# Issuing the sums, high parts and activation parts of a wide step ahead of the low parts of the step before it, in a fused attention, recurrence and feed-forward block

## The chip, the cores and the metric

The kernel runs on one core of a Trainium2 chip. A core has five engines with an instruction queue each: TensorE multiplies matrices, VectorE and ScalarE work on elements, GpSimd has little to do here, and SyncE issues most transfers from the chip's memory. Each engine works through its queue in order; across engines, an instruction waits on semaphores. The metric is the time of one execution in microseconds of the device, as the median of several runs.

## The reference, cut to what matters

One decoder layer on 256 positions of width 2048, in 32-bit floats. A norm, one combined projection, a dilated window attention and a gated recurrence, two branch projections with gates, an output projection and a residual; then

```
a = rmsnorm(h, norm_ffn_pre)
gt, up = split(a @ w_ffn_gate_up, [5632])      # 2048 x 11264
ff = (silu(gt) * up) @ w_ffn_down              # 5632 x 2048
h = h + rmsnorm(ff, norm_ffn_post)
```

The change lies in the feed-forward part alone, the last 690 us of the execution.

## The kernel before, in words

**Split products.** Every 32-bit number x is written as hi + lo, two numbers in TensorE's own 32-bit format. ScalarE makes `hi` by a copy into that format, VectorE makes `lo` as x - hi, and a product takes three matmuls: hi by hi, hi by lo and lo by hi. So each weight that TensorE uses costs a copy on ScalarE and a subtraction on VectorE first, the latter waiting for the former.

**Narrow and wide steps.** All projections up to the first block of the feed-forward go in chunks of 128 x 1024 elements (`load`, `split`, `multiply`, lines 210 to 272; the copy is L242, the subtraction L243). From the second gate/up block on the work goes in wide steps of 128 x 2048: two row blocks of 128 times two column groups of 512. There are ten gate/up blocks of 8 wide steps (`GATE_UP`) and two down blocks of 22 (`DOWN`).

**Plain and by7 steps.** A plain wide step is 24 matmuls of 512 columns. A by7 step computes its 2 by 2 block product with seven products instead of eight (21 matmuls) and pays for that with sums: three VectorE instructions over the weight (L310, L316, L317, tile `sum`), the high part of these in two halves (L315, L318, tile `w`), and a second pair of high and low parts for the plain weight (`dh` L320, `dl` L322), beside the low part of the sums (`wl` L321). A plain step has one high part (`w` L305) and one low part (`wl` L306). Steps 2, 4 and 6 of a gate/up block are by7, steps 4, 7, ..., 19 of the first down block and 3, 6, ..., 18 of the second.

**Activations.** In gate/up all activation parts exist beforehand. In down, `prep_act` makes them step by step: a high part on ScalarE (L410) and a low part on VectorE (L411, tile `a`), and for a by7 step four sums on VectorE (L379 to L383, tile `s`), their high part on ScalarE (L384) and their low part on VectorE (L385, tile `so`).

**Between blocks.** When a block's last by7 step is multiplied, `gather` (L363) spreads the four extra products: a copy on ScalarE (L367) and four additions on VectorE (L368 to L371, tile `e`). When the block is done, `evac_ffn` adds the banks (L1151), applies the gate's function (L1154) and multiplies gate and up (L1157); after step 1 of the next block TensorE transposes the outcome (L1117 in `turn_act`) into the activations of down. A down block's `evac_down` adds (L1191), squares and applies the gain (L1200).

**Buffers.** `raw` (a weight as loaded) has three buffers, `w` (high parts) three, `wl` (low parts) three, `sum`, `dh` and `dl` one each. A buffer is written again when all users of the tile that it held before are done, whatever the order in which the instructions were written down: step n's high part waits on ScalarE for TensorE to finish step n-3, and the load of step n waits on SyncE for the last reader of `raw` of step n-3, which is `wl` (L306) in a plain step and `dl` (L322) in a by7 step.

**Order.** It is written out by hand. For each wide step i the loop issues: `split_wide(i + 2)`, which holds all the preparation of step i + 2; the load of step i + 5 (two transfers of 512 KB); the matmuls of step i; `gather`, the next piece of the evacuation, the transposes, where they fall on this step. At the end the last three steps are multiplied side by side, so that the two halves of the output can be finished one after the other.

Of the kernel before, what the change touches and what calls it, by code (L numbers as in the profile page):

```python
# [13 lines left out]
F32 = mybir.dt.float32  # L14
F32R = mybir.dt.float32r
I32 = mybir.dt.int32
AF = mybir.ActivationFunctionType
OP = mybir.AluOpType

P = 128  # L20
# [57 lines left out]
def tile_hybrid_block(ctx: ExitStack, tc: tile.TileContext, t, out):  # L78
    nc = tc.nc
# [12 lines left out]
    def nm(s):  # L92
        serial[0] += 1
        return f"{s}_{serial[0]}"

    def rslot(s):
        return rpool.tile([P, 1024], F32R, tag="r", bufs=16, name=nm(s))
# [10 lines left out]
    def p3(s, dtype, n, bufs, tag=None):  # L108
        return act_pool[0].tile([P, n], dtype, tag=tag or s, bufs=bufs, name=nm(s))
# [73 lines left out]
    blocks, chunks, pairs = [], [], []  # L183
    wides, steps = [], []
# [21 lines left out]
    def parts(j):  # L206

        return (slice(0, 512), slice(512, 1024)) if j == 0 else (slice(0, 1024),)
# [19 lines left out]
    def wslot():  # L228
        return stream.tile([P, 2048], F32R, tag="w", bufs=N_SPLIT, name=nm("w"))

    def split(j, only=None):
        if j >= len(chunks):
            split_wide(j - len(chunks))
            return
        raw = chunks[j][2]
        if chunks[j][3] is None:
            w = wslot()
            chunks[j][3:] = [w[:, :1024], w[:, 1024:]]
        wh, wl = chunks[j][3:]
        for n, k in enumerate(parts(j)):  # L240
            if only in (None, n):
                nc.scalar.activation(wh[:, k], raw[:, k], AF.Copy)  # L242
                nc.vector.tensor_sub(wl[:, k], raw[:, k], wh[:, k].bitcast(F32))  # L243
# [48 lines left out]
            )  # L292
        steps[n][2] = raw

    def split_wide(n):

        if n >= len(steps):
            return
        b, i, raw = steps[n][:3]
        m, by7 = b.order[i]  # L300
        if b.prep:
            b.prep(m, by7)
        hi, lo = wslot(), p3("wl", F32R, 2048, 3)
        if not by7:
            nc.scalar.activation(hi, raw, AF.Copy)  # L305
            nc.vector.tensor_sub(lo, raw, hi.bitcast(F32))  # L306
            steps[n][3] = hi, lo
            return
        s, d = p3("sum", F32, 2048, 1), raw[:, 512:]
        nc.vector.tensor_sub(  # L310
            s[:, :1024].rearrange("p (a c) -> p a c", a=2),
            raw[:, 512:1536].rearrange("p (a c) -> p a c", a=2),
            raw[:, None, :512].to_broadcast([P, 2, 512]),
        )
        nc.scalar.activation(hi[:, :1024], s[:, :1024], AF.Copy)  # L315
        nc.vector.tensor_add(s[:, 1024:1536], raw[:, 512:1024], s[:, 512:1024])  # L316
        nc.vector.tensor_sub(s[:, 1536:], raw[:, 1536:], s[:, 1024:1536])  # L317
        nc.scalar.activation(hi[:, 1024:], s[:, 1024:], AF.Copy)  # L318
        dhi, dlo = p3("dh", F32R, 1536, 1), p3("dl", F32R, 1536, 1)
        nc.scalar.activation(dhi, d, AF.Copy)  # L320
        nc.vector.tensor_sub(lo, s, hi.bitcast(F32))  # L321
        nc.vector.tensor_sub(dlo, d, dhi.bitcast(F32))  # L322
        steps[n][3] = hi, lo, dhi, dlo
# [50 lines left out]
    def seven_sums(f, dst):  # L374

        s = ptile("s").rearrange("p (n t) -> p n t", n=4)
        a11, a12, a21, a22 = f[:, 0, :P], f[:, 1, :P], f[:, 0, P:], f[:, 1, P:]
        for o, x, c, y in ((0, a21, -1.0, a22), (1, s[:, 0, :], -1.0, a11)):
            nc.vector.scalar_tensor_tensor(  # L379
                out=s[:, o, :], in0=x, scalar=c, in1=y, op0=OP.mult, op1=OP.subtract  # L380
            )
        nc.vector.tensor_sub(s[:, 2, :], a11, a21)
        nc.vector.tensor_sub(s[:, 3, :], a12, s[:, 1, :])  # L383
        nc.scalar.activation(dst[:, 0], s, AF.Copy)  # L384
        nc.vector.tensor_sub(dst[:, 1], s, dst[:, 0].bitcast(F32))  # L385

    def sums_of(dst):
        return lambda n: (dst[:, 0, n, :], dst[:, 1, n, :])


    class Split:
# [14 lines left out]

        def put(self, n, src):

            x = self.slots[n]
            nc.scalar.activation(x[:, :, 0, :], src, AF.Copy)  # L410
            nc.vector.tensor_sub(x[:, :, 1, :], src, x[:, :, 0, :].bitcast(F32))  # L411
            self.there.add(n)

# [158 lines left out]
    def start():  # L572
        keep_warm(WARM)
        ps = aux()
        nc.tensor.transpose(ps[:, :16], rowg[:16], ident[:16, :16])
        nc.vector.tensor_copy(colg[:, :16], ps[:, :16])
        high, low = transpose_in(xt, colg, xT, 0, True)
        for kk in range(2):
            high(kk)
            low(kk)  # L580
            split(0, kk)
        keep_warm(BRIDGE)
        transpose_in(xt, colg, xT, 1)
        lanes[0].append(opening())
# [579 lines left out]
    fss, fz, fpost, parts_of, a7 = [], {}, [], {}, {}  # L1164
# [8 lines left out]
                t["norm_ffn_post"][:, j * 1024 : (j + 1) * 1024].to_broadcast([P, 1024]),  # L1173
            )

    def prep_act(m, by7):
        f = act_t[m // 2][:, m % 2 * 2 : m % 2 * 2 + 2, :]
        x = parts_of[m] = Split("a", 2)
        x.put(0, f)
        if by7:  # L1180
            dst = rslot("so").rearrange("p (z n t) -> p z n t", z=2, n=4)
            seven_sums(f, dst)
            a7[m] = sums_of(dst)
# [95 lines left out]
    for half in range(2):  # L1279
# [3 lines left out]
        for g in range(3):  # L1283
            c = 1024 * g + 512 * half
# [22 lines left out]
    for j in range(2):  # L1307
        add_wide_block(t["w_ffn_down"][0], (1024 * j, 1024 * j + 512), DOWN[j], act,
                       lambda m: a7[m], evac_down, prep=prep_act,
                       pre=begin_down if j == 0 else None, turn=3 if j == 0 else None)  # L1310
# [5 lines left out]
    for j in range(1, 4):  # L1316
        load_x(j)
        load(2 * j)
        if j < 3:
            load(2 * j + 1)  # L1320
    start()
    split(1)
    for j in range(N_RAW + 1, N_RAW + AHEAD):
        load(j)
    for i in range(len(chunks)):
        b, c = chunks[i][:2]
        if c == 0 and b.pre:
            b.pre()
        split(i + AHEAD)
        load(i + AHEAD + N_RAW)  # L1330
        multiply(i)
        if b.post:
            b.post(c)
        advance(evacs)
        if turns and type(turns[0]) is not list:
            advance(turns)
        for lane in lanes:
            advance(lane)
        if c == b.steps - 1:
            evacs.append(b.evac(b.banks))  # L1340
# [3 lines left out]
    for i in range(len(steps)):  # L1344
        b, c = steps[i][:2]
        now[0] = b
        if c == 0 and b.pre:
            b.pre()
        split_wide(i + AHEAD)
        load_wide(2 * (i + AHEAD + N_RAW // 2))  # L1350
        if i >= len(steps) - 3:
            continue
        multiply_wide(i)
        if c == b.last7:
            gather(b)
        advance(evacs)
        if c == b.turn:
            flush(evacs)
            turn_act(turns.popleft())
        if c == len(b.order) - 1:  # L1360
            evacs.append(b.evac(b))
            advance(evacs)
# [63 lines left out]
```

## Time and profile before

| what | value |
|---|---|
| median of 3 runs | 1753.54 us (1752.17 to 1753.55) |
| the profiled execution, own time | 1753.68 us |
| its span, first to last instruction | 1751.9 us |
| TensorE busy | 1730.3 us, 99% |
| VectorE busy | 1265.1 us, 72% |
| ScalarE busy | 885.0 us, 51% |
| loaded from memory | 322.40 MB, 185 GB/s over the span |

In the profile's rows, PE is TensorE's matmuls, PEld its loads of weights, DVE is VectorE, ACT ScalarE, SP SyncE. A timeline row gives start and duration in microseconds, engine, line, operation, the tile written and the tiles read, the shape, how many instructions are merged, and, in brackets, how long the engine had been idle and what ended that. Instructions overlap a little at their ends, so the next one can start some 0.08 us before the duration is over. A row by stretches gives the stretch, its length, then busy time and instructions of PE, PEld, DVE, ACT and POOL, the granted TensorE clock, the busy share of the DMA engines and GB/s.

### The profile page before, as it was taken

Reading aid. Unit: us, or ns where it says so; the run is one execution under the profiler, and the core shown is the slowest. Engines: PE = TensorE matmul, PEld = TensorE weight load, DVE = VectorE, ACT = ScalarE, POOL = GpSimd, SP = SyncE. Lnnn points to the kernel's source line nnn. Section 1 sums busy time; section 2 is a strip of 40 time slices with the busy share of each in tenths; the row PEclk is TensorE's granted clock in tenths of the full one; section 3 lists DMA queues with packets and bytes.
Section 4 is the critical chain, followed back from the end, with each engine's and each line's share of the span. In section 5 each row is a group of like instructions: output and inputs, shape, how many; then the busy total and the mean of one; then the engine's idle time right before and its main releaser. Section 6 shows DMA issues by size and latency. Waiting matters only on the chain.

```text
span 1751.9 us, 21592 instructions
## 1 busy us (share of the span) xinstructions
PE 1730.3 (99%) x8424; PEld 1449.0 (83%) x8424; DVE 1265.1 (72%) x1372; ACT 885.0 (51%) x1050; POOL 74.1 (4%) x54
## 2 busy tenths in 40 slices
PE   9999999999999999999999999999999999999997
PEld 7888888888888888888888877888888888878775
DVE  5657657877546775544565577888888888888887
ACT  6545445344444444454444465555555555565563
POOL 0002404300000000000000000000000000000000
PEclk9999999999999999999999999999999999999999
DMA  7655444455455554455555745555555555656553
GB/s 265 204 191 193 144 162 151 145 165 182 159 169 169 189 188 161 159 175 193 194 183 189 268 157 203 194 192 193 204 206 204 201 194 192 223 181 218 183 183 117
DMA packets 201223, 325.92 MB, mean 186 GB/s; under 512 B 10096, under 2 KB 76832, under 8 KB 201120
## 3 DMA queue, kind: packets, MB, share of 16 engines
q1 hardware_dynamic: 198848, 319.41, 54.2%
q10 hardware_dynamic: 2272, 5.12, 0.8%
q8 instruction: 66, 1.08, 0.2%
q14 instruction: 37, 0.30, 0.1%
HBM read 322.40 MB, written 2.10 MB: 185 GB/s over the span
## 4 chain that ended last, share of the span: by engine, by line
PE 82%; DVE 12%; ACT 3%; issue 2%; DMA 1%; POOL 0%; SPq 0%; DVEq 0%; ACTq 0%
PE acc L115 65%; PE aux L115 16%; DVE wl L306 3%; DVE wl L321 1%; DVE dl L322 1%; DVE a L411 1%; DVE sum L310 1%; ACT w L318 1%; DVE w L243 1%; DVE sum L317 0%; DVE sum L316 0%; ACT w L242 0%; DVE w L667 0%; ACT so L384 0%; DVE s L379 0%
## 5 line engine op out<-in xcount | busy, mean ns | idle before, releaser
L243 DVE TENSOR_TENSOR w<-raw,w 128x1024 fp32r<-128x1024 f32 (+1 forms) x353 | 444.2, 1260 | 366.4 <-ACT w L242 364.3
L242 ACT ACTIVATE w<-raw 128x1024 fp32r<-128x1024 f32 (+1 forms) x353 | 373.0, 1057 | 483.1 <-PE acc L115 472.1
L115 PE MATMUL acc<-w,xT 128*128 128x512 f32 x1728 | 407.9, 394 | 0.0
L115 PEld LDWEIGHTS acc<-w,xT 128*128 128x128 f32 x1728 | 325.1, 190 | 65.7 <-DVE w L243 0.3
L115 PE MATMUL acc<-xT,w 128*128 128x512 f32 (+1 forms) x2048 | 365.5, 340 | 0.0
L115 PEld LDWEIGHTS acc<-xT,w 128*128 128x128 f32 x2048 | 314.8, 189 | 46.1
L306 DVE TENSOR_TENSOR wl<-raw,w 128x2048 fp32r<-128x2048 f32 x82 | 187.4, 2285 | 19.9 <-ACT w L305 19.9
L305 ACT ACTIVATE w<-raw 128x2048 fp32r<-128x2048 f32 x82 | 156.4, 1908 | 59.0 <-PE aux L115 27.0
L115 PE MATMUL acc<-w,hT 128*128 128x512 f32 x622 | 182.5, 392 | 1.5 <-DVE w L243 1.2
L115 PEld LDWEIGHTS acc<-w,hT 128*128 128x128 f32 x622 | 115.8, 188 | 27.0 <-DVE w L243 2.5
L115 PE MATMUL aux<-w,hT 128*128 128x512 f32 x430 | 135.6, 389 | 0.0
L321 DVE TENSOR_TENSOR wl<-sum,w 128x2048 fp32r<-128x2048 f32 x42 | 96.3, 2292 | 47.3 <-ACT w L318 47.3
L115 PEld LDWEIGHTS aux<-w,hT 128*128 128x128 f32 x430 | 80.7, 188 | 16.8
L315 ACT ACTIVATE w<-sum 128x1024 fp32r<-128x1024 f32 x42 | 44.6, 1063 | 96.3 <-DVE sum L310 92.0
L115 PE MATMUL acc<-w,yT 128*128 128x512 f32 x384 | 88.0, 390 | 0.2 <-DVE w L243 0.2
L115 PEld LDWEIGHTS acc<-w,yT 128*128 128x128 f32 x384 | 71.9, 188 | 15.4 <-DVE w L243 0.6
L115 PE MATMUL acc<-w,a 128*128 128x512 f32 x268 | 83.7, 389 | 0.0
L115 PE MATMUL aux<-w,a 128*128 128x512 f32 x268 | 83.7, 389 | 0.0
L115 PE MATMUL aux<-wl,hT 128*128 128x512 f32 x215 | 83.6, 389 | 0.0
L115 PE MATMUL acc<-wl,hT 128*128 128x512 f32 x215 | 83.6, 389 | 0.0
L322 DVE TENSOR_TENSOR dl<-raw,dh 128x1536 fp32r<-128x1536 f32 x42 | 73.5, 1751 | 0.0
L320 ACT ACTIVATE dh<-raw 128x1536 fp32r<-128x1536 f32 x42 | 61.9, 1473 | 0.0
(263 smaller groups left out, 2016.9 us busy)
## 6 DMA issues: line engine op xcount, KB each, us to landing
raw<-in_w_in SPq DMA_DIRECT2D x271, 512.0 KB, 4.5
raw<-in_w_ffn_gate_up SPq DMA_DIRECT2D x176, 512.0 KB, 4.4
raw<-in_w_ffn_down SPq DMA_DIRECT2D x88, 512.0 KB, 4.9
raw<-in_w_mix_out SPq DMA_DIRECT2D x32, 512.0 KB, 4.9
raw<-in_w_attn_branch SPq DMA_DIRECT2D x16, 512.0 KB, 4.6
raw<-in_w_hgrn_branch SPq DMA_DIRECT2D x16, 512.0 KB, 4.6
hx<-in_x ACTq DMA_DIRECT2D x4, 512.0 KB, 9.9
x<-in_x SPq DMA_DIRECT2D x3, 512.0 KB, 10.4
```

The lines of the kernel that those rows point to most:

```text
L115: nc.tensor.matmul(ps, lhsT, rhs, start=start, stop=stop, skip_group_check=True)
L242: nc.scalar.activation(wh[:, k], raw[:, k], AF.Copy)
L243: nc.vector.tensor_sub(wl[:, k], raw[:, k], wh[:, k].bitcast(F32))
L305: nc.scalar.activation(hi, raw, AF.Copy)
L306: nc.vector.tensor_sub(lo, raw, hi.bitcast(F32))
L310: nc.vector.tensor_sub(s[:, :1024].rearrange("p (a c) -> p a c", a=2), raw[:, 512:1536].rearrange("p (a c) -> p a c", a=2), raw[:, None, : ...
L315: nc.scalar.activation(hi[:, :1024], s[:, :1024], AF.Copy)
L318: nc.scalar.activation(hi[:, 1024:], s[:, 1024:], AF.Copy)
L320: nc.scalar.activation(dhi, d, AF.Copy)
L321: nc.vector.tensor_sub(lo, s, hi.bitcast(F32))
L322: nc.vector.tensor_sub(dlo, d, dhi.bitcast(F32))
L411: nc.vector.tensor_sub(x[:, :, 1, :], src, x[:, :, 0, :].bitcast(F32))
```

## The change

`split_wide(n)` is cut in two. The new `front(n)` makes the activation's high part, the sums and the high parts of a step, and then the rest of its activation parts. `split_wide(n)` now makes `dh` of step n, then calls `front(n + 1)`, and then makes the low parts of step n. So the sums, high parts and activation parts of step n + 1 stand in the queues of VectorE and ScalarE ahead of the low parts of step n, and `front(i + 3)` is issued in the turn of step i, before the matmuls of step i. All three sums now come ahead of both halves of the high part, and in a by7 step of down the activation's low part and its seven sums come behind the weight's sums. The very first `front` is issued ahead of the split of the last narrow chunk. No buffer is added, the loads and the matmuls keep their order, and no instruction is added or taken away.

```diff
     def split(j, only=None):
+        if j >= len(chunks) - 1 and only is None:
+            split_wide(j - len(chunks))
         if j >= len(chunks):
-            split_wide(j - len(chunks))
             return
...
-    def split_wide(n):
+    def front(n):
 
         if n >= len(steps):
             return
         b, i, raw = steps[n][:3]
         m, by7 = b.order[i]
         if b.prep:
-            b.prep(m, by7)
-        hi, lo = wslot(), p3("wl", F32R, 2048, 3)
+            b.prep(m)
+        hi = wslot()
         if not by7:
             nc.scalar.activation(hi, raw, AF.Copy)
+            steps[n][3] = raw, hi
+        else:
+            s, d = p3("sum", F32, 2048, 1), raw[:, 512:]
+            nc.vector.tensor_sub(
+                s[:, :1024].rearrange("p (a c) -> p a c", a=2),
+                raw[:, 512:1536].rearrange("p (a c) -> p a c", a=2),
+                raw[:, None, :512].to_broadcast([P, 2, 512]),
+            )
+            nc.vector.tensor_add(s[:, 1024:1536], raw[:, 512:1024], s[:, 512:1024])
+            nc.vector.tensor_sub(s[:, 1536:], raw[:, 1536:], s[:, 1024:1536])
+            nc.scalar.activation(hi[:, :1024], s[:, :1024], AF.Copy)
+            nc.scalar.activation(hi[:, 1024:], s[:, 1024:], AF.Copy)
+            steps[n][3] = s, hi, d
+        if b.prep:
+            b.prep(m, by7)
+
+    def split_wide(n):
+
+        by7 = 0 <= n < len(steps) and steps[n][0].order[steps[n][1]][1]
+        if by7:
+            dhi = p3("dh", F32R, 1536, 1)
+            nc.scalar.activation(dhi, steps[n][3][2], AF.Copy)
+        front(n + 1)
+        if n >= len(steps) or n < 0:
+            return
+        if not by7:
+            raw, hi = steps[n][3]
+            lo = p3("wl", F32R, 2048, 3)
             nc.vector.tensor_sub(lo, raw, hi.bitcast(F32))
             steps[n][3] = hi, lo
             return
...
+        s, hi, d = steps[n][3]
+        dlo, lo = p3("dl", F32R, 1536, 1), p3("wl", F32R, 2048, 3)
         nc.vector.tensor_sub(lo, s, hi.bitcast(F32))
         nc.vector.tensor_sub(dlo, d, dhi.bitcast(F32))
...
-    def prep_act(m, by7):
+    def prep_act(m, by7=None):
+
         f = act_t[m // 2][:, m % 2 * 2 : m % 2 * 2 + 2, :]
-        x = parts_of[m] = Split("a", 2)
-        x.put(0, f)
+        if by7 is None:
+            parts_of[m] = Split("a", 2)
+            parts_of[m].high(0, f)
+            return
+        parts_of[m].low(0, f)
         if by7:
```

`put` of `Split` is cut into `high` (the copy on ScalarE) and `low` (the subtraction on VectorE) for this, and calls both where it is used otherwise.

More of the change, by code (lines that the diff above doesn't have):

```diff
@@ L308, in split_wide @@
             return
[L309 to L320, printed above, removed]
+        s, hi, d = steps[n][3]
+        dlo, lo = p3("dl", F32R, 1536, 1), p3("wl", F32R, 2048, 3)
         nc.vector.tensor_sub(lo, s, hi.bitcast(F32))
@@ L407, in put, with high, low @@
         def put(self, n, src):
+            self.high(n, src)
+            self.low(n, src)
+        def high(self, n, src):
+            nc.scalar.activation(self.slots[n][:, :, 0, :], src, AF.Copy)
+        def low(self, n, src):
             x = self.slots[n]
-            nc.scalar.activation(x[:, :, 0, :], src, AF.Copy)
             nc.vector.tensor_sub(x[:, :, 1, :], src, x[:, :, 0, :].bitcast(F32))
```

## The prediction, as put on record before the run

> **What bounds the kernel now.** I read the page first, then busy time by stretches, the chain of waits, and last the timelines of single engines around the steps that the change moves.
>
> ```profile
> span 1751.9 us, 21592 instructions
> ...
> PE acc L115 65%; PE aux L115 16%; DVE wl L306 3%; DVE wl L321 1%; DVE dl L322 1%; DVE a L411 1%; DVE sum L310 1%; ACT w L318 1%; DVE w L243 1%; DVE sum L317 0%; DVE sum L316 0%; ACT w L242 0%; DVE w L667 0%; ACT so L384 0%; DVE s L379 0%
> ```
> The chain belongs to TensorE for 81%; the VectorE lines in it are those that the change moves. By stretches, gate/up (1066 to 1501 us) and down (from 1501) differ:
>
> ```profile
> 1400.00:1500.00 100.00, 100.00 (x451) 82.99 (x450) 87.40 (x71) 54.61 (x46) 0.00 (x0) 1.00 0.60 204
> 1500.00:1600.00 100.00, 98.70 (x435) 80.25 (x434) 86.31 (x95) 57.17 (x57) 0.00 (x0) 1.00 0.61 200
> ```
> In gate/up TensorE is full: nothing can be won there. In down it waits, at one place per three steps:
>
> ```profile
> 1556.53 0.50 PE L115 MATMUL aux<-dl,a 128*128 128x512 f32 x1 [0.28 <-DVE dl L322]
> 1572.74 0.50 PE L115 MATMUL aux<-dl,a 128*128 128x512 f32 x1 [0.27 <-DVE dl L322]
> 1654.66 0.50 PE L115 MATMUL acc<-dl,a 128*128 128x512 f32 x1 [1.61 <-DVE dl L322]
> ```
> Three down steps take 16.21 us. Their 24+24+21 matmuls need, by the next row (48 in 10.88 us, 0.2267 each; 5.44 for a plain step, 4.76 for a by7 step), 15.64. So 0.57 is lost per cycle; nine such cycles, 0.5 at the first by7 step (a row further down) and 1.9 at 1654.66 (each is the idle time in brackets and 0.3 for the slower first matmuls behind it) make **7.5 us**: the most that a faster supply could give.
>
> ```profile
> 1458.62 10.88 PE acc L115 x48
> ```
> What holds the supply is VectorE's own order:
>
> ```profile
> 1557.00 2.28 DVE L306 TENSOR_TENSOR wl<-raw,w 128x2048 fp32r<-128x2048 f32 x1
> 1559.20 0.68 DVE L411 TENSOR_TENSOR a<-act,a 128x512 fp32r<-128x512 f32 x1
> ...
> 1562.01 0.68 DVE L411 TENSOR_TENSOR a<-act,a 128x512 fp32r<-128x512 f32 x1
> 1562.61 0.28 DVE L379 SCALAR_TENSOR_TENSOR s<-act 128x128 f32<-128x128 f32 x1
> ...
> 1564.32 0.69 DVE L385 TENSOR_TENSOR so<-s,so 128x512 fp32r<-128x512 f32 x1 [0.70 <-ACT so L384]
> 1564.93 1.22 DVE L310 TENSOR_TENSOR sum<-raw 128x1024 f32<-128x1024 f32 x1
> ...
> 1566.90 0.69 DVE L317 TENSOR_TENSOR sum<-raw,sum 128x512 f32<-128x512 f32 x1
> 1568.72 2.29 DVE L321 TENSOR_TENSOR wl<-sum,w 128x2048 fp32r<-128x2048 f32 x1 [1.13 <-ACT w L318]
> 1570.93 1.75 DVE L322 TENSOR_TENSOR dl<-raw,dh 128x1536 fp32r<-128x1536 f32 x1
> ```
> It is busy all the cycle but for 0.70 and 1.13, both waits for ScalarE. The change fills the 1.13.
>
> **The change, part by part.** No instruction is added or removed: VectorE, ScalarE and TensorE have as many as before. What moves is the place of three sums, a high part and an activation part: one low part earlier. Three things that the new place needs have to be asked: is the weight there, what stands behind, and who waits for that.
>
> *The weight (down).* A raw buffer is one of three, so step n's load starts when step n-3's last reader is done. For a by7 step that is `dl` of the by7 step before. What such a load takes shows where ScalarE waited for one:
>
> ```profile
> 1603.35 1.75 DVE L322 TENSOR_TENSOR dl<-raw,dh 128x1536 fp32r<-128x1536 f32 x1
> ```
> ```profile
> 1610.53 1.92 ACT L305 ACTIVATE w<-raw 128x2048 fp32r<-128x2048 f32 x1 [2.11 <-DMA raw<-in_w_ffn_down]
> ```
> From 1605.10 to 1610.53: 5.43 us. Before, two activation parts and two plain low parts (2.80 a pair), a third activation part and the seven sums stand behind `dl` ahead of the sums, 8.5 us in all, so the load is covered. After, one pair stands there: VectorE waits 2.6, and it works in order, so all behind the sums waits too: the activation's low part, the seven sums, and the plain low part that TensorE wants next. That closes a loop from one `dl` to the next: load 5.43, sums 2.58 (1564.93 to 1566.90, and 0.61), activation low part 0.60 (1562.01 to 1562.61), seven-sums with the trip to ScalarE 1.71 (1562.61 to 1564.32), their low part 0.61, plain low part 2.20 (1557.00 to 1559.20), activation low part 0.60, by7 low part 2.21 (1568.72 to 1570.93), `dl` 1.75. ScalarE's high part runs beside the activation sums. Sum **17.69 us** against 15.64 that TensorE needs: it waits 2.05 per cycle, now for the plain low part ahead of the by7 step. The load could be shorter or longer; the tile view of the raw buffers over three cycles bounds it:
>
> ```profile
> DMA to landing us min/median/max: 3.7/5.1/6.3
> ```
> A step has two such transfers, of half its weight each, and the slower counts. I take 5.43, since it is the same step's load at the same place, and keep 3.9 and 6.3 for the range: after the change the buffer before it is released only 4.5 us earlier, so transfers may overlap more.
>
> The Trainium skill, "DMA: Bandwidth & Descriptors", Anatomy of one DMA, fits a transfer (there on GpSimd's path) as 2.0 us plus bytes over 436 GB/s. By that estimate the megabyte takes 4.4 us, the loop 16.7, and the whole comes out some 10 us lower. The measured 5.43 does not agree and goes before it.
>
> *Gate/up, from block to block.* ScalarE's high part for step n+3 now stands ahead of `gather`'s copy, and it waits for the end of step n on TensorE (one of three w buffers).
>
> ```profile
> 1281.00 0.60 ACT L367 ACTIVATE e<-acc 128x512 f32<-128x512 f32 x1
> 1283.72 1.92 ACT L305 ACTIVATE w<-raw 128x2048 fp32r<-128x2048 f32 x1 [2.12 <-PE aux L115]
> ```
> ```profile
> 1283.17 0.68 DVE L368 TENSOR_TENSOR e<-acc,e 128x512 f32<-128x512 f32 x1
> ...
> 1285.96 2.28 DVE L306 TENSOR_TENSOR wl<-raw,w 128x2048 fp32r<-128x2048 f32 x1
> ...
> 1294.35 2.29 DVE L321 TENSOR_TENSOR wl<-sum,w 128x2048 fp32r<-128x2048 f32 x1 [1.12 <-ACT w L318]
> ...
> 1298.23 1.41 DVE L1157 SCALAR_TENSOR_TENSOR e<-e,r2c,e 128x512 f32<-128x512 f32 x2
> ```
> ```profile
> 1299.85 1.03 PE L1117 MATMUL aux<-ident,e 128*128 128x128 f32 x8
> ```
> The copy moves from 1281.00 to behind the high part (1283.72 + 1.9), so with its 0.60 the first gather add starts about 1286.2, not 1283.17: 3.0 later. From there to the end of the block's activation product (L1157, 1299.64) VectorE does the same work without the 1.12: 1.9 later in sum. TensorE's transposes wait for that product and started 0.2 after it: they are **1.7 us** late. This repeats in each of the nine transitions between gate/up blocks, since the next high part is again timed by TensorE: 9 x 1.7 = 15.3. Where the cover is there, the moves cost nothing: inside a block a low part stands ready about 1.2 us ahead of its step by the same counting (low part, load 5.43, sums, low part are 10.2 us for two steps of 10.2).
>
> *Into the first wide block.* The first wide high part (1.82) now stands ahead of the last narrow chunk's on ScalarE.
>
> ```profile
> 1070.26 2.36 DVE L243 TENSOR_TENSOR w<-raw,w 128x1024 fp32r<-128x1024 f32 x2 [0.25 <-ACT w L242]
> ```
> ```profile
> 1076.93 0.39 PE L115 MATMUL aux<-w,hT 128*128 128x512 f32 x1
> ```
> That chunk's low part ends about 1074.3, not 1072.6, and frees the third wide weight's buffer; with 5.43, 2.58 and a low part of 2.29, step 1 is ready at 1084.6. TensorE asks at 1076.93 + 5.44 + 0.23 = 1082.6: **2.0**.
>
> *Into down.* Again the copy stands behind a high part:
>
> ```profile
> 1495.59 1.92 ACT L305 ACTIVATE w<-raw 128x2048 fp32r<-128x2048 f32 x1 [1.60 <-PE acc L115]
> ```
> ```profile
> 1500.63 2.48 DVE L1151 TENSOR_TENSOR e<-acc,e 128x512 f32<-128x512 f32 x4
> 1505.23 0.69 DVE L411 TENSOR_TENSOR a<-act,a 128x512 fp32r<-128x512 f32 x1 [2.13 <-ACT a L410]
> ```
> ```profile
> 1524.11 0.50 PE L115 MATMUL aux<-dl,a 128*128 128x512 f32 x1 [0.24 <-DVE dl L322]
> ```
> The high part's 1.92 and the copy's 0.60 put the first gather add at 1498.15; with gather's 2.79 (1283.17 to 1285.96), an activation part 0.60 and a low part 2.20 the L1151 adds start at 1503.7; 4.6 later (as 1500.63 to 1505.23) the next activation part, then 11.9 (0.60, 2.20, product 1.33, sums 2.58, 0.60, 1.71, 0.61, low part 2.28): step 3 is ready at 1520.3. TensorE asks at 1517.5 (1524.11 less its wait of 0.5, the transposes' 0.9 and 23 matmuls): 2.8. In the cycle behind it those transposes fill 0.9 of the 2.05. Of the table load and of the gain's load that ScalarE issues there, nothing moves past the wide steps.
>
> *Sum for down.* Waits after: 2.8, 1.15, four of 2.05, 0.2 at the seam (six steps without by7 let VectorE catch up), two of 2.8 (each has one L1200 of 0.74 in its loop), three of 2.05: 24.1. Before 7.5. **+16.6.**
>
> ```profile
> 1636.33 0.74 DVE L1200 SCALAR_TENSOR_TENSOR fz<-e,r2c,fpost 128x512 f32<-128x512 f32 x1
> ```
>
> *The end.* The last gather copy now stands behind the last high part, which waits for its load:
>
> ```profile
> 1717.68 1.75 DVE L322 TENSOR_TENSOR dl<-raw,dh 128x1536 fp32r<-128x1536 f32 x1
> ...
> 1728.34 2.29 DVE L306 TENSOR_TENSOR wl<-raw,w 128x2048 fp32r<-128x2048 f32 x1
> ```
> ```profile
> 1730.68 0.50 PE L115 MATMUL acc<-wl,a 128*128 128x512 f32 x1 [0.66 <-DVE wl L306]
> ```
> The last low part ended 11.2 after `dl`; after, 5.43 + 1.82 + 0.64 + 2.79 + 2.29 = 13.0, while TensorE is 0.9 further behind `dl`: **+0.9**.
>
> Sum: 2.0 + 15.3 + 16.6 + 0.9 = 34.8. The profiled run took 1753.68 (span 1751.9 and 1.8 around it; the median is 0.14 less). 1753.7 + 34.8 = **1788.5 us**.
>
> **The rivals.**
>
> *The waits go and nothing takes their place.* Weights land ahead of the sums, and the copy's lateness is absorbed; TensorE is full in down too: 1753.7 - 7.5 = 1746.2, faster. For it: VectorE is idle 1.83 in 16.21, more than the 0.57 wanted. Against: the load row. It decides from the point at which a load comes back within 2.8 us of its buffer's release. 5%.
>
> *Only down and the first block lose.* The product L1157 keeps its cover, if TensorE's transposes have more slack than the 0.2 read here: 1788.5 - 15.3 = 1773.2. Against: 1299.64 and 1299.85. 12%.
>
> *Only the block transitions lose.* A loop of 16.2 instead of 17.7 would need a load of 3.9 us: down costs 2 or 3 at its entry, total near 1775. The row's 3.7 is one half of a weight, and both are needed. 8%.
>
> *Loads are slower*, 6.3: loop 18.6, 0.9 more in about ten cycles: 1798. 12%.
>
> *The clock falls.* Waits of 2 us and more come every 17.7 us. If half of the step behind each ran at half speed (2.7 us more), ten would cost 27: 1815. Against: the stretch 1640 to 1660, with a wait of 1.61, has the granted clock at 1.00. 3%. The Trainium skill, "TensorE: Matmul & The Clock Gate", Part 1, puts the fall behind an idle window of about 3.4 us; no wait worked out here is as long.
>
> ```profile
> 1640.00:1660.00 20.00, 18.39 (x81) 14.91 (x80) 18.07 (x19) 10.39 (x12) 0.00 (x0) 1.00 0.56 194
> ```
>
> **How the numbers follow.** The forecast has 60%. The low end 1770 lies under the two half cases, the high end 1799 over slow loads; outside lie the gain, the fallen clock and about a tenth more. Under 0.2% (3.5 us, about what a measurement can tell from no change) either way is left only for cases that cancel (a load near 3.9 with the transitions covered): 2%, out of the two half cases. Faster 5%, slower 93%.
>
> **What would show it.** In the profile after: the sums' first instruction idle some 2.6 us before it on a DMA, once per down cycle; TensorE's waits on `wl` of the plain low part (about 2 us, every 17.7 us), not on `dl`; TensorE idle about 1.7 us before each block's transposes; gather's copy right behind a plain high part. If the sums start without a wait for DMA, the down part is wrong; if the transposes follow without a gap, the gate/up part is.

## The result, and the profile after

The changed kernel takes 1798.58 us (median of 5 runs, 1797.08 to 1801.99), the kernel before 1753.54 in the same comparison: a ratio of 1.026, 95% interval 1.0245 to 1.0275, or 45 us more. The forecast was 34.8 us more, 1788.5. The profiled execution took 1797.08, with a span of 1794.9, 43.0 more than before.

The chain of waits on the page of the changed kernel:

```profile
PE 72%; DVE 15%; DMA 5%; issue 3%; ACT 3%; SPq 0%; POOL 0%; DVEq 0%; ACTq 0%
```

Before, TensorE carried 82% of the chain, VectorE 12% and loads 1%; now it is 72%, 15% and 5%. The waits of TensorE from 1066 us on, in the view that adds them up by what was waited for (us in total, times, longest):

```profile
PE aux L115 <- DVE wl L335: 11.9, 7, 2.7
PE acc L115 <- DVE wl L335: 11.6, 6, 3.7
PE aux L1142 <- DVE e L1182: 5.6, 10, 0.8
PE acc L1142 <- DVE e L1182: 4.5, 8, 0.8
PE aux L115 <- ACT act L1143: 2.2, 5, 0.4
PE acc L115 <- ACT act L1143: 2.0, 5, 0.4
```

L335 is now the low part of a plain step, L1142 the transposes, L1182 the product of gate and up, L1143 ScalarE's copies of the transposes. The waits for `dl`, which ended the idle time of down before, are gone. Three kinds took their place: for plain low parts (12 of the 13 in down), for the product ahead of the transposes (two rows for each of nine blocks), and one that the forecast does not have, for the copies behind the transposes.

**Between gate/up blocks.** ScalarE's timeline around the last block transition, first at the gather, then at the transposes (L306 high part of a plain step, L386 gather's copy, L317 and L318 the halves of a by7 step's high part):

```profile
1473.03 1.92 ACT L306 ACTIVATE w<-raw 128x2048 fp32r<-128x2048 f32 x1 [2.84 <-PE aux L115]
1474.85 0.57 ACT L386 ACTIVATE e<-acc 128x512 f32<-128x512 f32 x1
...
1491.96 1.06 ACT L317 ACTIVATE w<-sum 128x1024 fp32r<-128x1024 f32 x1 [3.09 <-DVE sum L310]
...
1494.30 1.07 ACT L1143 ACTIVATE act<-aux 128x512 f32<-128x512 f32 x2
```

The same transition on VectorE (L387 is the first gather add) and on TensorE:

```profile
1475.46 0.69 DVE L387 TENSOR_TENSOR e<-acc,e 128x512 f32<-128x512 f32 x1 [2.95 <-ACT e L386]
...
1489.30 1.41 DVE L1182 SCALAR_TENSOR_TENSOR e<-e,r2c,e 128x512 f32<-128x512 f32 x2
```

```profile
1490.10 0.33 PE L1142 MATMUL aux<-ident,e 128*128 128x128 f32 x1 [0.79 <-DVE e L1182]
1490.77 0.98 PE L1142 MATMUL aux<-ident,e 128*128 128x128 f32 x7 [0.33 <-DVE e L1182]
...
1494.93 0.50 PE L115 MATMUL aux<-w,so 128*128 128x512 f32 x1 [0.45 <-ACT act L1143]
```

Read them in order. Gather's copy begins the moment the plain high part is done, and that high part had waited 2.84 us for TensorE. VectorE stood idle for the copy, 2.95 us. The product ends late, so TensorE waits for it twice, before its first transpose and before its second. Then, 4 us later, a by7 product wants a bank that ScalarE empties only at 1494.30, because the two halves of the high part stand ahead of the copies and wait for the sums, which VectorE makes after the late product. Before, the copies followed the transposes directly, as at the same transition in the kernel before, where the transposes start at 1469.34:

```profile
1469.98 1.09 ACT L1118 ACTIVATE act<-aux 128x512 f32<-128x512 f32 x2 [2.98 <-PE aux L1117]
```

From one block's first transpose to the next is 44.68 us (1132.65 to 1490.10 in eight), before 42.39 (1130.19 to 1469.34): 2.29 more each.

**Down.** VectorE over one step, with `dl` (L341), which is the raw buffer's last reader, the plain low part, and the next sums:

```profile
1562.92 1.75 DVE L341 TENSOR_TENSOR dl<-raw,dh 128x1536 fp32r<-128x1536 f32 x1
...
1565.19 2.29 DVE L335 TENSOR_TENSOR wl<-raw,w 128x2048 fp32r<-128x2048 f32 x1
1570.00 1.23 DVE L310 TENSOR_TENSOR sum<-raw 128x1024 f32<-128x1024 f32 x1 [2.52 <-DMA raw<-in_w_ffn_down]
```

The chain of waits over the same stretch runs through the loop itself, from `dl` to the issue on SyncE, the transfer and the sums:

```profile
1562.92 1.76 DVE dl L341
...
1564.74 0.37 SPq L290
...
1565.15 4.72 DMA raw<-in_w_ffn_down
```

From `dl`'s end to the sums are 5.3 us here and 5.5 in the next cycle. TensorE's waits in the first down block come at 1542.34, 1560.26 and then every 17.6 to 17.7 us; in the second block they are 18.7, 18.7, 17.9 and 17.8 us apart:

```profile
1560.26 0.50 PE L115 MATMUL aux<-wl,a 128*128 128x512 f32 x1 [1.05 <-DVE wl L335]
...
1682.64 0.50 PE L115 MATMUL acc<-wl,a 128*128 128x512 f32 x1 [3.66 <-DVE wl L335]
...
1701.35 0.79 PE L115 MATMUL acc<-wl,a 128*128 128x512 f32 x1 [2.74 <-DVE wl L335]
...
1720.09 0.50 PE L115 MATMUL acc<-wl,a 128*128 128x512 f32 x1 [1.19 <-DVE wl L335]
...
1737.96 0.50 PE L115 MATMUL acc<-wl,a 128*128 128x512 f32 x1 [1.90 <-DVE wl L335]
...
1755.73 0.50 PE L115 MATMUL acc<-wl,a 128*128 128x512 f32 x1 [0.17 <-DVE wl L335]
```

Two of the second block's loads took longer than the 4.7 to 5.0 us of the others in this chain:

```profile
1668.58 6.07 DMA raw<-in_w_ffn_down
...
1706.25 5.86 DMA raw<-in_w_ffn_down
```

**The clock.** Behind two of these waits the granted clock fell, in the view by stretches (the clock is the third column from the end):

```profile
1682.60:1684.00 1.40, 1.36 (x6) 1.12 (x7) 1.40 (x3) 1.40 (x2) 0.00 (x0) 1.00 0.11 38
1702.00:1704.00 2.00, 2.00 (x6) 1.60 (x5) 2.00 (x1) 0.59 (x2) 0.00 (x0) 0.50 0.66 183
...
1740.00:1742.00 2.00, 2.00 (x6) 1.57 (x5) 2.00 (x2) 0.00 (x0) 0.00 (x0) 0.50 0.95 314
```

Summed over the stretches from 1702 to 1706 and 1738 to 1744, the lost share of the clock is 3.1 us. Before, the clock was 1.00 in every stretch read from 1650 to 1710. The slow matmuls did not lengthen the cycles that they fell into: TensorE still waited for the next plain low part at the end of both, 1.19 us at 1720.09 and 0.17 at 1755.73, and the second cycle took 17.77 us, beside 17.58 to 17.73 in the first block. They took the place of waiting.

Where the 43.0 us lie, by the starts of the same instructions in the two traces: 1.0 up to the first transposes (1087.8 and 1088.8), 21.1 more up to down's first matmul (1500.83 and 1522.95), about 19.6 in down and 1.3 at the end.

### The profile page after: what moved, and what is told of

Its sections match the earlier page's. It is cut to its first block, busy times and chain, and to the rows that moved or that the text cites. A ratio compares the mean times of both kernels' runs of the same rounds, so it can differ in the third digit from the quotient of the medians.

```text
span 1794.9 us, 21633 instructions
## 1 busy us (share of the span) xinstructions
PE 1740.1 (97%) x8424; PEld 1449.1 (81%) x8424; DVE 1264.8 (70%) x1372; ACT 885.7 (49%) x1050; POOL 73.0 (4%) x54
## 4 chain that ended last, share of the span: by engine, by line
PE 72%; DVE 15%; DMA 5%; issue 3%; ACT 3%; SPq 0%; POOL 0%; DVEq 0%; ACTq 0%
PE acc L115 60%; PE aux L115 12%; DVE wl L335 3%; DMA raw<-in_w_ffn_down 3%; DMA raw<-in_w_ffn_gate_up 2%; DVE wl L340 2%; DVE dl L341 2%; DVE sum L310 1%; DVE e L1176 1%; ACT w L306 1%; DVE sum L315 1%; DVE a L436 1%; DVE w L244 1%; ACT w L243 1%; DVE w L692 0%
## 5 line engine op out<-in xcount | busy, mean ns | idle before, releaser
L306 ACT ACTIVATE w<-raw 128x2048 fp32r<-128x2048 f32 x82 | 156.9, 1914 | 146.6 <-PE aux L115 61.0
L335 DVE TENSOR_TENSOR wl<-raw,w 128x2048 fp32r<-128x2048 f32 x82 | 187.5, 2286 | 24.7 <-ACT w L306 24.7
L317 ACT ACTIVATE w<-sum 128x1024 fp32r<-128x1024 f32 x42 | 44.6, 1063 | 146.9 <-DVE sum L310 108.7
L310 DVE TENSOR_TENSOR sum<-raw 128x1024 f32<-128x1024 f32 x42 | 51.4, 1223 | 47.8 <-DMA raw<-in_w_ffn_down 27.7
L115 PEld LDWEIGHTS acc<-w,yT 128*128 128x128 f32 x384 | 71.9, 188 | 15.3 <-DVE w L244 0.5
L341 DVE TENSOR_TENSOR dl<-raw,dh 128x1536 fp32r<-128x1536 f32 x42 | 73.6, 1754 | 0.0
```

The costliest lines, as they stand in the source:

```text
L115: nc.tensor.matmul(ps, lhsT, rhs, start=start, stop=stop, skip_group_check=True)
L310: nc.vector.tensor_sub(s[:, :1024].rearrange("p (a c) -> p a c", a=2), raw[:, 512:1536].rearrange("p (a c) -> p a c", a=2), raw[:, None, : ...
```

## The experiments

Two theories stood against each other. A, the forecast's: in gate and up ScalarE's order makes the gather late, in down a loop through the raw buffer's load holds VectorE. B: putting the sums ahead of the low parts costs on VectorE wherever it is done. Ratios are to the kernel before, run beside each kernel; on its 1753.5 us, 0.1% is 1.75 us.

| kernel | median us | ratio, 95% interval |
|---|---|---|
| changed kernel | 1798.58 | 1.026 [1.0245, 1.0275] |
| early front in gate/up only | 1777.64 | 1.0135 [1.012, 1.015] |
| early front in down only | 1773.25 | 1.0115 [1.0099, 1.013] |
| early front of plain steps only | 1789.62 | 1.0209 [1.0193, 1.0224] |
| `dl` ahead of `wl` | 1814.42 | 1.035 [1.0333, 1.0367] |
| gather's copy first | 1773.5 | 1.0127 [1.0111, 1.0144] |
| transposes' copies first | 1792.43 | 1.0234 [1.0218, 1.0249] |
| half of the by7 load left out | 1784.41 | 1.0182 [1.0167, 1.0197] |
| order inside the by7 step | 1744.7 | 0.9959 [0.9945, 0.9973] |

### The change in gate/up only, and in down only

```diff
+    def early(n):
+        return 0 <= n < len(steps) and bool(not steps[n][0].prep)
...
-        front(n + 1)
...
+            if early(n + 1):
+                front(n + 1)
...
```

Steps that are not early are prepared as before. `prep` is set in down alone; the second kernel has the same without `not`.

> The early front is kept for gate/up steps alone; the down steps are prepared in the order of before. Theory A (in gate/up, gather's copy stands behind a high part that waits for TensorE, and the transposes' copies stand behind the high part of step 4; in down, the load): entry into the first wide block 1.6, nine transitions of 2.3 us (44.68 a block in the profile after against 42.37), down as before: 1753.5 + 22 = 1775 us. Rival B (the sums ahead of a low part make every low part late on VectorE, whatever the copies and loads do): the cost goes with the number of by7 steps, 30 in gate/up of 42, so 45 x 30/42 = 32: 1786 us.

> The early front is kept for the down steps alone. Theory A: the load's loop of 17.7 us per cycle, the entry into down and the end, 20 to 22 us in sum: 1773 to 1776 us, with VectorE's sums waiting for a DMA in each down cycle. Rival B: 12 of the 42 by7 steps, 45 x 12/42 = 13: 1766 us.

Measured 1777.64 and 1773.25, so 24 and 20 us more than before: for the first 2.6 us over A's 1775 and 8 under B's 1786, for the second inside A's range. The two add up to the whole (2.5% of 2.6%). TensorE's waits from 1066 us on, with the change in down only:

```profile
PE acc L115 <- DVE wl L385: 10.9, 5, 3.2
PE aux L115 <- DVE wl L385: 8.2, 5, 2.7
```

Only the waits for plain low parts are there. With the change in gate/up only there are these, beside the old ones of down for `dl`:

```profile
PE aux L1191 <- DVE e L1231: 5.6, 10, 0.8
PE acc L1191 <- DVE e L1231: 4.5, 8, 0.8
...
PE acc L115 <- ACT act L1192: 2.2, 5, 0.5
PE aux L115 <- ACT act L1192: 2.2, 5, 0.4
```

The same totals as in the changed kernel. Each half of the loss has its own cause.

### Only plain steps early

```diff
+    def early(n):
+        return 0 <= n < len(steps) and not steps[n][0].order[steps[n][1]][1]
...
-        front(n + 1)
...
+        if early(n + 1):
+            front(n + 1)
...
```

A by7 step's sums and high parts are then made in its own turn, directly ahead of its low parts.

> Only the plain steps have their high part (and, in down, activation part) issued ahead of the low part of the step before; by7 steps with their sums are prepared in the order of before. Theory A: at a gate/up block's end the next plain high part still stands ahead of gather's copy, while VectorE's wait of 1.12 stays, so the transposes come about 2.8 us late (3.0 less 0.2), nine times 2.8 = 25, and some 3 at the entry of down and at the end: 1782 us (1775 to 1786); a down cycle stays at 16.2. Rival B: no sum is moved, so no change: 1753.5 us.

Measured 1789.62: B, by which the cost is in the by7 steps' sums, falls, since those stand where they stood. But A had 1782, and the loss is larger than worked out. It lies at the transitions: block to block is 45.77 us (1133.46 to 1499.61 in eight), 3.37 more than before, while down and the end add under 4. TensorE and VectorE at one transition (L357 the by7 low part, L1201 the product):

```profile
1315.74 0.33 PE L1161 MATMUL aux<-ident,e 128*128 128x128 f32 x1 [2.01 <-DVE e L1201]
```

```profile
1311.06 2.29 DVE L357 TENSOR_TENSOR wl<-sum,w 128x2048 fp32r<-128x2048 f32 x1 [1.12 <-ACT w L354]
...
1314.94 1.41 DVE L1201 SCALAR_TENSOR_TENSOR e<-e,r2c,e 128x512 f32<-128x512 f32 x2
```

Gather's copy is as late as in the changed kernel, for the plain high part is still ahead of it; but the 1.12 us in which VectorE waits for the second half is back on the way to the product. The transposes wait 2.01 where they waited 0.79, 1.22 more: about that 1.12.

Most of what A's sum lacked is the granted clock. Five of the eight blocks take 45.2 us, 2.8 more than before, as worked out; three take 46.7 to 46.8, and in these three alone the clock fell to about half speed 1 to 2 us behind the first transpose (in 1226 to 1228, 1318 to 1320 and 1454 to 1458 us), though the waits ahead of the transposes, 2.01 and then 0.33, are the same in all nine. The stretch with the three falls:

```profile
1200.00:1500.00 300.00, 283.87 (x1244) 232.14 (x1242) 239.91 (x198) 148.48 (x123) 0.00 (x0) 0.98 0.54 183
```

Three falls of 1.6 us make 4.8. Here they are lost, for no wait of TensorE behind them becomes shorter by it.

### `dl` ahead of `wl` in a by7 step

```diff
-        nc.vector.tensor_sub(lo, s, hi.bitcast(F32))
         nc.vector.tensor_sub(dlo, d, dhi.bitcast(F32))
+        nc.vector.tensor_sub(lo, s, hi.bitcast(F32))
```

The raw buffer is released some 2.3 us earlier.

> As the changed kernel, but in a by7 step the low part dl is made ahead of the low part wl of the sums, so that the last reader of the raw buffer is done 2.2 us earlier; VectorE has the same work. Theory A: the loop of a down cycle, 17.7 us, becomes 5.43 + 2.58 + 0.60 + 1.71 + 0.61 + 2.20 + 0.60 + 1.75 = 15.5, under TensorE's 15.64, so the cycles cost nothing more (16.2 or less each) while gate/up keeps its 22 us: 1773 us (1769 to 1778). Rival B: the same work in the same order ahead of each plain low part: 1798 us.

Measured 1814.42, neither. In gate/up the edit brings a wait of its own. `dl` needs `dh`, which ScalarE makes behind the two gate functions, and now VectorE stands for it ahead of the product:

```profile
1318.44 1.76 DVE L340 TENSOR_TENSOR dl<-raw,dh 128x1536 fp32r<-128x1536 f32 x1 [1.57 <-ACT dh L328]
```

Block to block is 47.13 us, 4.73 more than before, with a granted clock of 0.97 over gate/up: seven of the eight blocks have a fall of the clock and take 47.1 to 47.3 us, the one without takes 46.4. In down, the release is earlier, and the transfer is not:

```profile
1563.98 1.75 DVE L340 TENSOR_TENSOR dl<-raw,dh 128x1536 fp32r<-128x1536 f32 x1
...
1573.87 1.23 DVE L310 TENSOR_TENSOR sum<-raw 128x1024 f32<-128x1024 f32 x1 [3.13 <-DMA raw<-in_w_ffn_down]
```

SyncE issued the load at 1565.80, right behind `dl`, and the sums still had to wait until 1573.87: 8.1 us from release to use, against 5.3 to 5.5 in the changed kernel. The load before it had been issued at 1563.53. Both together, 2.1 MB, took the 10.3 us up to the sums, and the DMA engines were busy for 0.78 of that:

```profile
1563.50:1574.00 10.50, 10.48 (x43) 8.58 (x44) 7.37 (x6) 4.51 (x6) 0.00 (x0) 0.84 0.78 246
```

So the earlier release put two loads on top of each other, and nothing was gained. The edit was no clean test of the loop; the half load below is a better one.

### Gather's copy ahead of the early front

```diff
...
+        if i < len(steps) - 3:
+            multiply_wide(i)
+            if c == b.last7:
+                first_copy(b)
         split_wide(i + AHEAD)
         load_wide(2 * (i + AHEAD + N_RAW // 2))
...
-        multiply_wide(i)
```

`first_copy` is gather's copy on ScalarE; the additions stay where they are. VectorE's queue is the same as in the changed kernel.

> The changed kernel, but ScalarE's copy of the gather (and the products ahead of it) is issued ahead of the next step's early front, so that it no longer stands behind a high part that waits for TensorE; what VectorE does, and in which order, stays. Theory A (the loss in gate and up comes from ScalarE's order at the nine block transitions, 2.3 us each by the periods 42.37 and 44.68): 9 x 2.3 = 20.7 us less than the changed kernel's 1798.6, so 1777.9 (1774 to 1782), with transposes about 42.4 us apart. Rival B (the loss comes from the sums ahead of the low parts on VectorE): VectorE's order is unchanged, so 1798.6 (1795 to 1802).

Measured 1773.5, 1.27% over before instead of 2.6%: half a us under A's 1774 to 1782, and B falls, since nothing moved on VectorE. ScalarE and TensorE now:

```profile
1453.28 0.60 ACT L384 ACTIVATE e<-acc 128x512 f32<-128x512 f32 x1
1456.00 1.92 ACT L306 ACTIVATE w<-raw 128x2048 fp32r<-128x2048 f32 x1 [2.12 <-PE aux L115]
```

```profile
1472.12 1.03 PE L1143 MATMUL aux<-ident,e 128*128 128x128 f32 x8
```

The copy stands ahead of the high part that waits 2.12 us; the eight transposes follow the last matmul without a wait, and from block to block it is 42.37 us (1133.14 to 1472.12 in eight) as before the change. The waits for the transposes' copies are gone with it, all but one of 0.31 us in the first block, though these still stand behind the halves: the product ends early enough. Down's first matmul is at 1503.61, 2.8 us later than before the change and not 22.1. What is left of the loss lies in down and at the entry.

### The transposes' copies ahead of the early front

```diff
-        split_wide(i + AHEAD)
-        load_wide(2 * (i + AHEAD + N_RAW // 2))
+        turning = c == b.turn and i < len(steps) - 3
+        if not turning:
+            split_wide(i + AHEAD)
+            load_wide(2 * (i + AHEAD + N_RAW // 2))
...
             turn_act(turns.popleft())
+        if turning:
+            split_wide(i + AHEAD)
+            load_wide(2 * (i + AHEAD + N_RAW // 2))
```

> The changed kernel, but in the one step of each block that turns the product, TensorE's transposes and ScalarE's two copies of them are issued ahead of the next front, so that the copies no longer stand behind the high parts of the sums. Theory A (of the 2.3 us that a transition loses, about 0.6 is TensorE's wait for a bank that these copies empty late, and 1.7 the gather's late copy): 9 x 0.6 = 5.3 us less than 1798.6, so 1793.3 (1790 to 1796). If the halves of the sums, now about 1.1 us later, are themselves late for TensorE, nothing is won: 1798.6. Rival B (VectorE's order): unchanged, 1798.6.

Measured 1792.43, 1.0234, against 1.026: 4.6 us less, as A had it, though the two intervals just overlap, so that the rows carry the reading. ScalarE at a transition, then TensorE:

```profile
1485.45 1.09 ACT L1143 ACTIVATE act<-aux 128x512 f32<-128x512 f32 x2 [2.48 <-PE aux L1142]
```

```profile
1484.21 0.33 PE L1142 MATMUL aux<-ident,e 128*128 128x128 f32 x1 [0.79 <-DVE e L1182]
```

The copies run as soon as the transposes are done, ahead of the first half (L317, at 1486.43), and TensorE's waits on L1143 are gone; the 0.79 ahead of the transposes stays. Block to block is 43.97 us (1132.44 to 1484.21 in eight): 1.58 more than before instead of 2.29. So a transition's loss splits into 1.6 for the late gather and 0.7 for the late copies.

### Half of the by7 load left out

```diff
         for g, col in enumerate(b.cols):
+            if b.prep and b.order[i][1] and i > 2 and g == 1:
+                nc.gpsimd.memset(raw[:, 1024:], 0.01)
+                continue
```

> The changed kernel, but in the down projection the steps with seven products load only one of their two 512 KB halves; the other half of the buffer is filled with a constant by GpSimd, so this part of the weights is left out of the result. What the engines compute on, and in which order, stays. Theory A (in down a loop through the buffer, released by the last low part, then the load of about 5.4 us, then the sums, takes 17.7 us and TensorE only 15.6): the load falls to about 3 us, the loop to under 15.6, and down loses neither the 19.5 us that the change added nor the some 7 us that the kernel before lost there: 1798.6 - 19.5 = 1779, down to 1772. Rival B (VectorE's order): 1798.6 (1795 to 1802).

In the twelve by7 steps of down this kernel leaves out the second 512 KB, and GpSimd writes a constant there, so these weights are missing from its output. Measured 1784.41, 1.0182: about 14 us less than the changed kernel, where A had 19.5 or more and B none. VectorE in down, its instructions as long as before (L344 `dl`, L313 the sums):

```profile
1562.50 1.75 DVE L344 TENSOR_TENSOR dl<-raw,dh 128x1536 fp32r<-128x1536 f32 x1
...
1568.19 1.23 DVE L313 TENSOR_TENSOR sum<-raw 128x1024 f32<-128x1024 f32 x1 [1.14 <-DMA raw<-in_w_ffn_down]
...
1584.52 1.23 DVE L313 TENSOR_TENSOR sum<-raw 128x1024 f32<-128x1024 f32 x1 [1.24 <-DMA raw<-in_w_ffn_down]
```

From `dl`'s end to the sums are 3.9 us instead of 5.4, and a cycle takes 16.33 us instead of 17.6 to 17.7. The cycle shrinks by what the load shrinks, so the load is in the loop. What was off is the expected size: with half of the bytes it is 3.9 us and not 3, so the loop is still longer than the 15.64 that TensorE needs.

### The aim of the change, inside the step

The idle time that the change wanted to fill can be filled without moving anything across steps. In the kernel before, within a by7 step of down, the activation's low part and seven sums come behind the weight's sums, and `so`'s low part behind the low part of the sums:

```diff
+        rest = b.prep(m, True) if b.prep else None
...
         nc.vector.tensor_sub(lo, s, hi.bitcast(F32))
+        if rest:
+            rest()
         nc.vector.tensor_sub(dlo, d, dhi.bitcast(F32))
...
```

> The kernel before, with its order of steps; only inside a down step with seven products VectorE does the sums, the activation's low part and the activation's sums, then the low part of the sums, then the low part of the activation's sums, so that its two waits for ScalarE (0.70 and 1.13 us) fall behind other work. Theory A (the aim of the change can be had without moving the front across steps, since then neither the gather's copy nor the loads come later): the 7.5 us that TensorE waits in down go, 1753.5 - 7.5 = 1746 (1744 to 1750). If the loads or ScalarE hold the down loop at its old length all the same: 1753.5 (1752 to 1755).

Measured 1744.7 beside 1751.96 for the kernel before in that comparison: 0.9959, interval 0.9945 to 0.9973, 7.3 us less. VectorE in the by7 step, with no bracket on any row, and TensorE over the stretch of down (busy time is its second number):

```profile
1562.84 2.29 DVE L324 TENSOR_TENSOR wl<-sum,w 128x2048 fp32r<-128x2048 f32 x1
1565.04 0.69 DVE L392 TENSOR_TENSOR so<-s,so 128x512 fp32r<-128x512 f32 x1
1565.64 1.75 DVE L327 TENSOR_TENSOR dl<-raw,dh 128x1536 fp32r<-128x1536 f32 x1
```

```profile
1501.00:1700.00 199.00, 199.00 (x883) 164.92 (x882) 180.88 (x192) 123.17 (x124) 0.00 (x0) 1.00 0.62 204
```

TensorE is full in down, and no wait of TensorE is left from 1066 us on. This order beats both kernels: 7.3 of the 7.5 us that were to be had are had, and none of the prices of the change is paid.

## Why the forecast was right, and where it was wrong

**Direction and places: right.** The trace after shows each sign that the forecast named: the sums idle 2.5 to 3.7 us on a load once per down cycle, TensorE waiting on the plain `wl` and no longer on `dl`, gaps ahead of the transposes (0.79 and 0.33, where about 1.7 was named), gather's copy right behind a plain high part. The experiments show the two big causes separately: gather's copy alone brings gate/up back to its old period, and the down cycle follows the load's length.

**Gate/up: the step that failed.** This is the largest part of the difference. "9 x 1.7 = 15.3" covers what follows from the late gather, and that part held: 1.6 per transition with the transposes' copies moved out of the way. But the measured loss was 21.1, 2.3 each. The working stopped at the start of the transposes ("TensorE's transposes wait for that product ... they are 1.7 us late") and did not ask what stands ahead of ScalarE's two copies behind them. These copies were put at nothing without a reason. It is again the moved high part, in its second form: the halves that wait for the sums. That is 0.7 per transition, 6.3 in nine.

**Down: the loop right, the load too small in two cycles.** The cycles of 17.61, 17.73 and 17.58 us in the first block answer to "Sum 17.69 us". Down lost 19.6 us, not 16.6, and most of the difference lies in the second block. The term that was mis-sized is the load, for which the working took 5.43 us in every cycle. In two cycles of the second block the sums began 6.7 and 6.5 us behind the end of `dl`, because the transfers took 6.07 and 5.86 us: 2.3 of the 3.0. The wait at 1682.64 is 3.66, with 0.3 of slow first matmuls behind it, for 2.8, and the cycle that ends at 1720.09 took 18.74 for 17.69. The rest is spread over the other cycles in tenths. Why these two loads took longer stays open; the loads at the same two places of that block also took 5.7 us each in the run with the change in down only and in the run with gather's copy first.

**The clock: missed, and without a price in down.** The rival "The clock falls" was held against a single row at 1.00 behind a wait of 1.61, and given 3% for ten falls and 27 us. There were two falls, 3.1 us of lost clock, and they fell inside a loop that VectorE and the load hold, so that TensorE's next wait was shorter by about as much. The run with the change in down only shows the same: a cycle with a fall (0.50 in 1574 to 1576 us) took 17.73 us between TensorE's waits, its neighbours 17.76 and 17.75, and only the wait at its end differed, 0.19 for 1.81. So "2.7 us more" for each fall would not have followed in down; in gate/up, with plain steps early, a fall did cost 1.6.

**Entry and end.** 1.0 for 2.0 and 1.3 for 0.9. With gate/up 5.8 and down 3.0 over, these make up the 8.2 between 34.8 and the 43.0 of the spans. The remaining 2 us of the difference lie between the profiled execution and the medians.

**The rivals.** That waits go and nothing takes their place, and that only one of the two parts loses, are out by the first two experiments. Slower loads, 6.3, are partly true, in two cycles and not in ten. In the first block the load was 5.3 to 5.6 us from release to use. The forecast's remark that transfers may overlap when the buffer before is released shortly ahead is what the run with `dl` first shows.

## What to carry to other kernels

When a step is moved forward in a queue, list everything that now stands behind it on that engine, and for each of these who waits for it, to the end of the chain and not to the first waiting engine: here one moved high part delayed two different copies, and only the first was priced. A prefetch that is issued earlier needs its buffer earlier; if the buffer's last reader is in the step just ahead, the load's whole latency enters the loop. Before a slower matmul is priced, see whether its engine waits at the end of the same cycle: where it does, the delay only shortens that wait. Before work is moved across steps, see whether the idle time can be filled by work of the same step.

## What the runs showed of the hardware

**Half a load is not half the time.** From release to use, 1 MB took 5.3 to 5.8 us in eight cycles of the changed kernel (6.5 and 6.7 in the other two), and 512 KB 3.9 to 4.1 in most. If the time goes straight with the size, which two sizes cannot show, the second half costs about 1.4 us, and some 2.5 us do not depend on the size; this is an estimate from these two. The Trainium skill, "DMA: Bandwidth & Descriptors", Anatomy of one DMA, has for transfers issued by GpSimd a fixed part of about 2.0 us and 436 GB/s, which by estimate makes 1.2 us of the second half; the estimate from the runs is of the same shape and larger in both terms.

**Two loads issued 2.3 us apart.** The second took 8.1 us from release to use (1565.8 to 1573.9, `dl` first); issued 4.5 us behind the load before it (1560.3 and 1564.7, changed kernel), it took 5.3. This is one place in each trace.

**The clock does not go by the length of a wait alone.** In the changed kernel it fell to 0.50 behind waits of 2.74 and 1.90 us, and stayed at 1.00 behind one of 3.66. With plain steps early, nine transitions had the same two waits, 2.01 and 0.33 us, and the clock fell behind three of them. The Trainium skill, "TensorE: Matmul & The Clock Gate", Part 1, has the slow state come after an idle window of about 3.4 us, and says of the window that it runs freely and does not start anew with a kernel. That a wait's place in such a window matters would fit these rows; no run here shows the window. That only a window without any work lets the clock fall does not fit a fall behind 1.90 us.
